# One pool for split weights and activations, a lookahead that depends on the place, and three pieces of work moved, in a two-layer hybrid encoder

## The chip, the cores and the metric

The kernel runs on one core of a Trainium2 chip. The time is the device time in microseconds (us) of one execution; the time of a kernel is the median of its runs. TensorE (PE) multiplies matrices, VectorE (DVE), ScalarE (ACT) and GpSimd (POOL) work element by element, and SyncE (SP) only issues DMAs. PEld is TensorE's loading of weights into its array, which runs beside its matmuls. PSUM, where the matmuls accumulate, has 8 banks of 128 x 512 float32; everything else lives in SBUF.

## The reference, cut to what matters

The input is 256 tokens of 1024 float32 values; two layers run one after the other, each with a gated feed-forward network (FFN), two kinds of attention with a common projection, and a second FFN.

```python
def swiglu(h, w_gate, w_up, w_down):
    return (jax.nn.silu(h @ w_gate) * (h @ w_up)) @ w_down

def reference(x, ...):
    for l in range(2):
        x = x + 0.5 * swiglu(rms_norm(x, ffn1_norm[l]), ffn1_w_gate[l], ffn1_w_up[l], ffn1_w_down[l])
        h = rms_norm(x, mix_norm[l])
        qa, ka, va, qb, kb, vb = jnp.split(h @ w_in[l], SPLITS, axis=-1)
        ...
        out_a = windowed_gqa_sink(qa, ka, va, sink[l], slopes_a)      # softmax with a sink, 8 heads, keys up to 128 away
        out_b = differential_attention(qb, kb, vb, lam, slopes_b)     # softmax1 - lam * softmax2, 4 heads
        out_b = rms_norm(out_b, diff_subln[l]) * (1.0 - lam_init)
        x = x + jnp.concatenate([out_a, out_b], axis=-1) @ w_out[l]
        x = x + 0.5 * swiglu(rms_norm(x, ffn2_norm[l]), ffn2_w_gate[l], ffn2_w_up[l], ffn2_w_down[l])
    return rms_norm(x, final_norm)
```

The hidden width of an FFN, `D_FF`, is 2816. `lam` comes from four short vectors per layer; `slopes` are powers of two.

## The kernel before, in words

**Split operands.** A float32 matrix product is made from three products of a faster type (float32r, written fp32r in the profile): each operand is split into `hi`, its rounded value, and `lo`, what the rounding left, and x·w is taken as xh·hi + xl·hi + xh·lo. So each piece of a product is three matmuls into one PSUM bank (`tokens`, L495; `prod`, L589). ScalarE makes `hi` by a copy, VectorE `lo` by a subtraction (`emit_split`, L175).

**Weight steps.** All weights are listed in advance, in the order of their use, as `specs`: one step is 1 MB, in an FFN 4 blocks of 128 rows by 512 columns. SP loads a step into one of 6 raw buffers (`emit_dma`, L147; the tiles `raw`). It is split in two halves (a half split), each into two buffers `w` of 128 x 2 x 512, from 14 such buffers (L181). `weights()` (L232) is called where a step is used. It first calls `ahead`, which issues all loads, preparations and splits up to half split 2i + HALVES, where i is the step and HALVES is 14 // 2 - 1 = 6, less a number that may be given. When the second half of a step is first touched, `part` (L166) lets `ahead` go one half further, unless the step is `held`. `ahead` is thus what places the splits in the queues of ScalarE and VectorE, among the other work.

**The order.** Every engine keeps the order in which the program issues (class `Kept`, L40), except in the first part of `mix`, where `kept[0]` is False and a scheduler chooses it. An instruction that waits holds up everything behind it on its engine.

**One FFN pass** (`ffn`, L567; four of them: two layers by two). Token blocks are t = 0, 1 of 128 tokens, and the 2816 hidden columns are groups n = 0 to 4 of 512 and a rest of 256. A group computes gate and up (each over 8 blocks of 128 rows of the input), silu by ScalarE, their product `h` by VectorE (`hidden`, L583); the next group turns `h` (`turn`, L634: transposes by TensorE, then a split as above) and multiplies it by the down weights of its group into four banks `accs` that stay for the whole pass (`down`, L648). So 4 of the 8 banks are left for the rest. Groups 0 and 1 are plain. Groups 2, 3 and 4 (`SEVEN`) get gate and up together by seven products in place of eight, in the manner of Strassen (`by_seven`, L599): m1, m7, p2, p3, p5, p6 and p4 in this order, with the halves of h's down product between. Sums of weights for them come from a gather-add DMA issued by POOL (`gather`, L125: c into b, b into a) and from additions by VectorE (`plus`, L130). Sums of x come from `make_sums` (L332), called in pieces through `next(sums, None)` in group 1. The differences of the products (`put`, L604, tiles `tmp`) are VectorE's; g1, the last of them that frees a bank, reads the bank of p4 (L623).

**Work around it.**

- `operands` (L311) splits x, transposed and scaled by the gain, into `xs`; `copies` (L322) makes a plain copy of the same banks by eight ScalarE operations, needed only by `make_sums`. It comes at the end of `take_x(2)` in the first pass (L430) and of `Residual.late(2)` in the others (L565), both called as `before(2)` in `ffn` (L662), before group 0's second half. The banks of the transposes are held until then.
- `constants` (L452) issues eight small DMAs, an iota and small operations on POOL, for the attention. `attention_constants` (L475) is the rest of these: a transpose of the gains into `gcol`, distances, and from `lsum` by an Exp on ScalarE (`lex`) the `nlam`: one transpose by TensorE, 11 operations of VectorE, one of ScalarE. It is `ffn`'s `aside`, called in the first pass at the start of n = 3 (L669). In the last pass `aside` is `final_gain` (L969), a load by SP and a memset.
- `blk` (L77) takes buffers for activations (xs, h, turned h, queries, keys) from the pool `s4` of 14, of the same size in bytes as a `w`.
- `mix` (L739) projects, does both attentions and the output projection; `ffn_end` and `ffn_close` (L700, L720) finish a pass and begin the next norm.

Of the kernel before, what the change touches and what calls it, by code (L numbers as in the profile page):

```python
# [10 lines left out]
F32R = mybir.dt.float32r  # L11
# [14 lines left out]
BIG = 1e33  # L26

AHEAD = 10
N_RAW, N_W = 6, 14
N_S4 = 14  # L30
SEVEN = (2, 3, 4)


# [1 line left out]
def trunk(ctx: ExitStack, tc: tile.TileContext, x, n1, g1, u1, d1, nm, w_in, sink,  # L35
# [31 lines left out]
    def nm_(s):  # L67
        uid[0] += 1
        return f"{s}_{uid[0]}"
# [90 lines left out]
    class Split:  # L160
# [5 lines left out]
        def part(self, k, c=slice(None), h=None):  # L166

            if h is None:
                h, k = divmod(k, 2)
            if h and not self.held:  # L170
                self.held = True
                ahead(2 * self.i + 1 + HALVES)
            return [t[:, k, c] for t in self.parts[h]]

    def emit_split(i, j):  # L175
        s = specs[i]
        raw = raws[s.src]
        if j == 0:
            loaded[i] = Split(i)
        shape = (P, 8, P) if s.n == 256 else (P, 2, 512)  # L180
        hi, lo = [wp.tile(list(shape), F32R, tag="w", bufs=N_W, name=nm_("w")) for _ in range(2)]  # L181
        loaded[i].parts.append((hi, lo))
        if s.n == D:
            raw = raw[:, :, j * 512:(j + 1) * 512]
        elif i in paired:
            raw = raw.rearrange("p k (s c d) -> p c k s d", s=2, c=2)[:, j]
            hi, lo = [t.rearrange("p k (s d) -> p k s d", s=2) for t in (hi, lo)]
        elif s.n == 256:
            raw = raw[:, :, j * P:(j + 1) * P]
        else:  # L190
            raw = raw[:, 2 * j:2 * j + 2]
        m = shape[1] // 2 if i < 2 or i in fine else shape[1]
        for a in range(0, shape[1], m):
            r_, h_, l_ = [t[:, a:a + m] for t in (raw, hi, lo)]
            act.copy(h_, r_)
            dve.tensor_tensor(l_, r_, f(h_), op=ALU.subtract)
            if i < 2:
                yield
        if j == 1:
            for k in s.free:  # L200
                raws.pop(k)
# [3 lines left out]
        for j in range(2):  # L205
            yield from emit_split(i, j)

    HALVES = N_W // 2 - 1
    at = dict(use=0, dma=2, prep=2, split=4)

    def ahead(n):

        n = min(n, 2 * len(specs) - 1)
        while True:
            if at["split"] <= n and at["prep"] > at["split"] // 2:
                for _ in emit_split(*divmod(at["split"], 2)):
                    pass
                at["split"] += 1
            elif at["prep"] <= min(n // 2 + 1, len(specs) - 1) and at["dma"] > at["prep"] and \
                    (specs[at["prep"]].prep is None or at["split"] >= 2 * at["prep"]):  # L220
                if specs[at["prep"]].prep is not None:
                    specs[at["prep"]].prep()
                at["prep"] += 1
            elif at["dma"] < min(at["use"] + AHEAD, len(specs)) and (specs[at["dma"]].moves is None or len(raws) < N_RAW):
                if specs[at["dma"]].moves is not None:
                    for _ in emit_dma(at["dma"]):
                        pass
                at["dma"] += 1
            else:
                break  # L230

    def weights(less=0, held=False):  # L232

        i = at["use"]
        at["use"] += 1
        if i > 1:
            ahead(2 * i + HALVES - less)
        w = loaded[i]
        w.held = held
        return w  # L240
# [168 lines left out]
    def take_x(k):  # L409

        g, u = early
        if k == 0:
            for j in (0, 1):
                sl = norm.turn(j)
                next(g)
                norm.operands(j, sl)
                next(u)
        elif k == 1:
            for e in (g, u, g, u):
                next(e)  # L420
            norm.pair(2)
            ahead(5)
            norm.pair(3)
        elif k == 2:
            ahead(7)
            for t in range(2):
                for h in range(2):
                    norm.squares(t, h * 512, 512)
            norm.stats()
            norm.copies()  # L430
            constants()

    grow = const.tile([NG - 16, P], F32, name="grow")
# [108 lines left out]
    class Residual:  # L542
# [14 lines left out]
        def late(self, k):  # L557

            if k == 1:
                self.nxt.pair(2)  # L560
                self.nxt.pair(3)
                self.squares(1)
            elif k == 2:
                self.nxt.stats()
                self.nxt.copies()  # L565

    def ffn(norm, aside=None, before=None, final=False):  # L567
        def silu(out_, acc, t):
# [30 lines left out]
        def by_seven(h, g):  # L599


            flat = lambda: tmp().rearrange("p a n -> p (a n)")

            def put(o, x, y, op):  # L604
                dve.tensor_tensor(o, x, y, op=op)
                return o

            m1, m7 = flat(), flat()
            act.copy(m1, prod(norm.quarter(0, 0), weights()))
            act.copy(m7, prod(norm.summed(2), weights(held=True)))  # L610
            hT = turn(h, 2)
            p2 = prod(norm.quarter(0, 1), weights())
            g0 = put(flat(), p2, m1, ALU.add)
            p3 = prod(norm.summed(3), weights())
            silu(g0, g0, 0)
            down(hT, g - 1, 0, weights())
            h = blk(F32)
            p5 = prod(norm.summed(0), weights())
            p6 = prod(norm.summed(1), weights())
            u2 = put(flat(), p6, m1, ALU.subtract)  # L620
            u3 = put(m7, m7, u2, ALU.add)
            p4 = prod(norm.quarter(1, 1), weights())
            g1 = put(m1, p4, u3, ALU.subtract)  # L623
            w = weights()
            silu(g1, g1, 1)
            put(u3, u3, p5, ALU.subtract)
            put(u2, u2, p5, ALU.subtract)
            put(u2, u2, p3, ALU.add)
            up(h, u2, g0, 0)
            up(h, u3, g1, 1)  # L630
            down(hT, g - 1, 1, w)
            return h
# [19 lines left out]
        gs, us = [bank(), bank()], [bank(), bank()]  # L652
        if before is None:
            before = norm.late
        before(0)
        ws = (weights(), weights(2))
        for k in (0, 2):
# [8 lines left out]
        h = hidden(g, us)  # L666
        for n in range(1, NGRP):
            sums = norm.make_sums() if n + 1 == min(SEVEN, default=0) else iter(())
            if n == 3 and aside is not None:  # L669
                aside()  # L670
            if n in SEVEN:
                h = by_seven(h, n)
                continue
            gs = [bank(), bank()]
            tokens(gs, norm.xs, weights(), 0)
            hT = turn(h, 2)
            tokens(gs, norm.xs, weights(), 4)
            g = gate(gs)
            next(sums, None)
            us = [bank(), bank()]  # L680
            for k0 in (0, 4):
                tokens(us, norm.xs, weights(), k0)
                next(sums, None)
            h = hidden(g, us)
            for hh in range(2):
                down(hT, n - 1, hh, weights())
                if hh == 0:
                    next(sums, None)

        gu = [bank(), bank()]  # L690
        tokens(gu, norm.xs, weights(), 0)
# [8 lines left out]
    def ffn_end(parts, last):  # L700

        accs, hT, rest = parts
        hT = [None] * (2 * (NGRP - 1)) + hT
        hE = []
        w = {0: weights()}

        def group(h, order, a=None, c=slice(None), first=0):
            tokens(a or accs[h], hT, w[h], G4, first=first, last=last[h], order=order, cols=c)

        def tail(h, order=BY_TOKENS, a=None, c=slice(None)):  # L710
            tokens(a or accs[h], [None] * (2 * NGRP) + hE, w["rest"], 4 * NGRP, last=last[h], order=order, cols=c, h=h)

        group(0, [(k, t) for k in range(3) for t in range(2)])
        hE.extend(rest())
        group(0, [(3, t) for t in range(2)])
        w["rest"] = weights()
        w[1] = weights(2)
        return group, tail

    def ffn_close(parts, nxt):  # L720
        group, tail = ffn_end(parts, (FC - 1, G4 + 3))
        res = Residual(nxt, parts[0])
        group(1, [(0, t) for t in range(2)])
        tail(0)
        for t in range(2):
            res.add(0, t)
        tail(1)
        ahead(2 * at["use"] - 2 + HALVES)
        group(1, [(1, t) for t in range(2)])
        for j in range(2):  # L730
            nxt.pair(j)
        res.squares(0)
        group(1, [(2, t) for t in range(2)])
        group(1, [(3, t) for t in range(2)])
        for t in range(2):
            res.add(1, t)
        nxt.late = res.late
# [318 lines left out]
```

## Time and profile before

| | |
|---|---|
| runs | 944.03, 944.5 and 947.19 us; median 944.5 |
| the profiled execution | 946.16 us |
| its span in the trace | 944.4 us |
| granted TensorE clock, mean | 0.993 |
| TensorE in the pieces `ps<-w,s` of 512 columns | 2754 matmuls, 645.4 us, 392 ns each |
| split of weights on VectorE, `w<-raw,w` | 440 operations, 464.1 us, 1094 ns each |
| split of weights on ScalarE, `w<-raw` | 440 operations, 399.1 us, 949 ns each |
| DMA | 194.59 MB, mean 206 GB/s |

The profile is of one execution. Its span runs from the first to the last instruction; the device time holds a little more around it. A matmul's record lasts longer than the distance to the next one, because matmuls are pipelined, so the records overlap and a busy share near the whole span does not say how fast the matmuls follow each other. In a group's line stand engine, line, operation, output tile <- input tiles, and their shapes; every instruction goes through the helper at L50, so tiles, not lines, tell the work apart. Behind a group may stand, in brackets, how long the engine was idle before it and what ended that.

### The profile page before, as it was taken

The numbers are of one execution on the slowest core, as the hardware profiler recorded it, in microseconds if no ns is written. First come the engines' busy times: TensorE is split into PE (matmuls) and PEld (weight loads), VectorE is DVE, ScalarE is ACT, GpSimd is POOL, SyncE is SP. The second block draws the span as 40 slices with busy tenths as digits, with TensorE's granted clock in tenths as the row PEclk, the third lists the DMA queues.
The fourth block names the chain that finished last, engine by engine and source line by source line (L and its number), as shares of the span: only waits on it lengthen the run. The fifth ranks groups of instructions, "written<-read, shape, count | busy, mean of one in ns | idle before, by whom it ended". The sixth has DMA issues, their size and how long they took to land.

```text
span 944.4 us, 12947 instructions
## 1 busy us (share of the span) xinstructions
PE 924.9 (98%) x4796; PEld 783.5 (83%) x4796; DVE 762.2 (81%) x1066; ACT 582.2 (62%) x901; POOL 53.6 (6%) x73
## 2 busy tenths in 40 slices
PE   8999899999999999999999999999999999999997
PEld 6788688899898888887888888878999888888876
DVE  6679999869955678999866799996796556799993
ACT  6756576467735756675575566665676475575662
POOL 0500010000000000000000010000000000010001
PEclk9999899999999999999999999999999999999999
DMA  9986797836424875897658498886652348499821
GB/s 336 345 222 182 218 277 255 271 120 194 134 90 134 233 213 141 263 295 265 239 178 235 122 278 223 259 296 195 194 161 90 130 157 249 103 286 268 254 93 45
DMA packets 110895, 194.59 MB, mean 206 GB/s; under 512 B 3566, under 2 KB 31280, under 8 KB 110832
## 3 DMA queue, kind: packets, MB, share of 16 engines
q1 hardware_dynamic: 96816, 167.27, 52.2%
q0 software_dynamic: 12928, 25.46, 15.1%
q10 hardware_dynamic: 1088, 1.05, 0.3%
q8 instruction: 37, 0.61, 0.3%
q14 instruction: 26, 0.21, 0.1%
HBM read 192.71 MB, written 1.05 MB: 205 GB/s over the span
## 4 chain that ended last, share of the span: by engine, by line
PE 83%; DVE 7%; DMA 5%; issue 2%; ACT 2%; ACTq 0%; DVEq 0%; POOLq 0%; POOL 0%
PE ps L50 83%; DVE w L50 5%; DMA raw<-in_ffn_w_up_dram 3%; DVE tmp L50 1%; ACT w L50 1%; DMA raw<-in_ffn_w_gate_dram 1%; DMA xk<-in_x_dram 1%; DVE s L50 1%; DVE raw L50 0%; ACT s L50 0%; ACT junk L50 0%; ACT tmp L50 0%; ACT L50 0%; ACTq L50 0%; DVE xk L50 0%
## 5 line engine op out<-in xcount | busy, mean ns | idle before, releaser
L50 PE MATMUL ps<-w,s 128*128 128x512 f32 (+1 forms) x2754 | 645.4, 392 | 7.1 <-DVE tmp L50 3.5
L50 PEld LDWEIGHTS ps<-w,s 128*128 128x128 f32 x2754 | 514.0, 189 | 115.2 <-DVE tmp L50 4.8
L50 DVE TENSOR_TENSOR w<-raw,w 128x1024 fp32r<-128x1024 f32 (+1 forms) x440 | 464.1, 1094 | 86.9 <-ACT w L50 84.1
L50 ACT CAST w<-raw 128x1024 fp32r<-128x1024 f32 (+1 forms) x440 | 399.1, 949 | 189.7 <-PE ps L50 97.1
L50 PE MATMUL ps<-w,q 128*128 128x512 f32 x432 | 101.9, 389 | 0.0
L50 PEld LDWEIGHTS ps<-w,q 128*128 128x128 f32 x432 | 81.1, 188 | 16.8
L50 PE MATMUL ps<-s,w 128*128 128x256 f32 x672 | 84.0, 285 | 0.0
L50 PEld LDWEIGHTS ps<-s,w 128*128 128x128 f32 x672 | 81.7, 192 | 1.1
L50 DVE TENSOR_TENSOR raw<-raw,raw 128x1024 f32<-128x1024 f32 x48 | 56.5, 1218 | 0.0
L50 POOL DMA_DIRECT2D raw<-in_ffn_w_up_dram x24 | 31.0, 1293 | 364.4 <-DVE tmp L50 157.2
L50 DVE TENSOR_TENSOR s<-ps,s 128x512 fp32r<-128x512 f32 x48 | 31.0, 685 | 18.1 <-ACT s L50 18.1
L50 ACT ACTIVATE s<-ps,gcol 128x256 fp32r<-128x256 f32 (+1 forms) x80 | 31.3, 476 | 20.7 <-PE ps L50 20.7
L50 ACT CAST s<-ps 128x512 fp32r<-128x512 f32 x48 | 26.1, 594 | 28.1 <-PE ps L50 28.1
L50 PE MATMUL ps<-ident,s 128*128 128x128 f32 x304 | 39.9, 273 | 1.7 <-DVE s L50 1.7
L50 PEld LDWEIGHTS ps<-ident,s 128*128 128x128 f32 x304 | 35.0, 141 | 6.9 <-ACT w L50 1.8
L50 ACT ACTIVATE s<-s,negm 128x256 f32<-128x256 f32 x64 | 31.8, 500 | 6.6 <-DVE negm L50 6.6
L50 ACT ACTIVATE tmp<-tmp,r 128x512 f32<-128x512 f32 x24 | 17.3, 722 | 29.2 <-DVE tmp L50 29.2
L50 PE MATMUL ps<-w,v 128*128 128x512 f32 x144 | 34.6, 389 | 0.0
L50 PEld LDWEIGHTS ps<-w,v 128*128 128x128 f32 x144 | 27.2, 189 | 5.7
L50 DVE SCALAR_TENSOR_TENSOR s<-ps,gcol,s 128x256 fp32r<-128x256 f32 x48 | 20.3, 479 | 14.4 <-ACT s L50 14.3
L50 DVE TENSOR_TENSOR tmp<-ps,tmp 128x512 f32<-128x512 f32 x36 | 24.6, 684 | 0.0
L50 DVE TENSOR_TENSOR tmp<-tmp,ps 128x512 f32<-128x512 f32 x36 | 23.6, 683 | 0.4
(107 smaller groups left out, 407.0 us busy)
## 6 DMA issues: line engine op xcount, KB each, us to landing
raw<-in_ffn_w_down_dram SPq DMA_DIRECT2D x44, 1024.0 KB, 5.2
raw<-in_ffn_w_gate_dram SPq DMA_DIRECT2D x39, 1024.0 KB, 5.4
raw<-in_ffn_w_up_dram SPq DMA_DIRECT2D x39, 1024.0 KB, 5.1
raw<-in_ffn_w_up_dram POOLq DMA_DIRECT2D x24, 1024.0 KB, 10.7
raw<-in_w_in_dram SPq DMA_DIRECT2D x14, 1024.0 KB, 5.7
raw<-in_ffn_w_gate_dram SPq DMA_DIRECT2D x8, 512.0 KB, 6.7
raw<-in_ffn_w_up_dram SPq DMA_DIRECT2D x8, 512.0 KB, 7.7
raw<-in_w_in_dram SPq DMA_DIRECT2D x8, 512.0 KB, 5.1
```

The costliest lines, as they stand in the source:

```text
L50: ins = issue(*a, **k)
```

## The change

- One pool of 28 buffers, tag `s4`, takes the place of the 14 buffers `w` and the 14 of `s4`: split weights and activations share it. The number of bytes is the same.
- `HALVES` = 6 becomes `look[0]`: 6 at the end of a pass and in `mix`, 8 in an FFN up to group 2, 7 in group 3 and 6 in group 4.
- In group 4 the steps of p6, p4 and the second down product are asked for with `less`, so that `ahead` goes only to half splits 2i+5, 2i+4 and 2i+3, and those of p6 and p4 are `held`. Splits that stood ahead of g1 in the queues come behind it, some after the calls that follow.
- `norm.copies()` goes from the end of `before(2)` to group 1, behind the turn of group 0's h.
- `aside()` goes from the start of n = 3 to group 1, behind the first down product of group 0 and the piece of `make_sums` that follows it. In the first pass that is `attention_constants`, in the last `final_gain`.

```diff
-N_RAW, N_W = 6, 14
-N_S4 = 14
+N_RAW, N_S4 = 6, 28
+IN_FFN, IN_MIX = 8, 6
...
-                ahead(2 * self.i + 1 + HALVES)
+                ahead(2 * self.i + 1 + look[0])
...
-        hi, lo = [wp.tile(list(shape), F32R, tag="w", bufs=N_W, name=nm_("w")) for _ in range(2)]
+        hi, lo = [s4.tile(list(shape), F32R, tag="s4", name=nm_("w")) for _ in range(2)]
...
-    HALVES = N_W // 2 - 1
+    look = [IN_MIX]
...
-            ahead(2 * i + HALVES - less)
+            ahead(2 * i + look[0] - less)
...
             norm.stats()
-            norm.copies()
             constants()
...
                 self.nxt.stats()
-                self.nxt.copies()
...
-            p6 = prod(norm.summed(1), weights())
+            late = g == max(SEVEN)
+            p6 = prod(norm.summed(1), weights(look[0] - 5 if late else 0, late))
             u2 = put(flat(), p6, m1, ALU.subtract)
             u3 = put(m7, m7, u2, ALU.add)
-            p4 = prod(norm.quarter(1, 1), weights())
+            p4 = prod(norm.quarter(1, 1), weights(look[0] - 4 if late else 0, late))
             g1 = put(m1, p4, u3, ALU.subtract)
-            w = weights()
+            w = weights(look[0] - 3 if late else 0)
...
+        look[0] = IN_FFN
         before(0)
...
-            if n == 3 and aside is not None:
-                aside()
             if n in SEVEN:
+                look[0] = IN_FFN - max(0, n - 2)
                 h = by_seven(h, n)
                 continue
...
             hT = turn(h, 2)
+            norm.copies()
...
                 down(hT, n - 1, hh, weights())
                 if hh == 0:
                     next(sums, None)
+                    if aside is not None:
+                        aside()
+                        aside = None
...
+        look[0] = IN_MIX
         w = {0: weights()}
...
-        ahead(2 * at["use"] - 2 + HALVES)
+        ahead(2 * at["use"] - 2 + look[0])
```

## The prediction, made before the changed kernel ran

> **What bounds the kernel now.** I read the page first, then the waits of TensorE alone, then busy time by stage, and last the timeline around each gap. The page says that TensorE sets the time:
>
> ```profile
> PE 924.9 (98%) x4796; PEld 783.5 (83%) x4796; DVE 762.2 (81%) x1066; ACT 582.2 (62%) x901; POOL 53.6 (6%) x73
> ```
>
> The waits of TensorE are few (total, count, longest, in us):
>
> ```profile
> PE ps L50 <- DVE tmp L50: 3.5, 3, 1.2
> PE ps L50 <- ACT tmp L50: 3.5, 1, 3.5
> ...
> PE ps L50 <- DVE s L50: 1.7, 2, 1.4
> ```
>
> So no change to the buffers can win more than these gaps and what the clock loses after them. The windows (length, busy of each engine with its instructions, granted clock, DMA share, GB/s) show that loss, and how full VectorE is:
>
> ```profile
> 39.60:43.00 3.40, 3.40 (x10) 2.62 (x9) 3.34 (x4) 1.40 (x2) 1.30 (x1) 0.51 1.05 401
> 109.30:114.70 5.40, 5.40 (x13) 4.24 (x14) 5.39 (x6) 5.19 (x7) 0.00 (x0) 0.51 0.00 0
> 340.00:350.00 10.00, 10.00 (x46) 8.29 (x45) 7.88 (x10) 4.98 (x6) 1.28 (x1) 1.00 0.70 154
> 430.00:440.00 10.00, 10.00 (x45) 7.98 (x44) 9.94 (x10) 6.39 (x7) 0.00 (x0) 1.00 0.66 226
> ```
>
> In dense stretches matmuls of 512 columns start 0.227 us apart (24 in 5.44 us). At a clock of 0.51 only 13 start in 5.40 us where 24 would: 11 x 0.227 = 2.5 us lost. In 39.6 to 43.0 it is 10 for 15: 1.1 us. VectorE has a fifth of its time free in group 1 (340 to 350) and none in group 4.
>
> **The three kinds of gap.** First pass, end of group 0:
>
> ```profile
> 26.22 3.00 ACT L50 ACTIVATE s<-ps,gcol 128x256 f32<-128x256 f32 x8
> ...
> 32.42 1.27 ACT L50 ACTIVATE tmp<-ps,r 128x512 f32<-128x512 f32 x2
> ...
> 36.94 1.40 DVE L50 SCALAR_TENSOR_TENSOR s<-ps,hr,tmp 128x512 f32<-128x512 f32 x2
> ...
> 37.83 0.30 PE L50 MATMUL ps<-ident,s 128*128 128x128 f32 x1 [1.43 <-DVE s L50]
> ```
>
> The eight copies of x stand ahead of the silu; the transposes wait for h. First pass, after group 2, where the constants sit:
>
> ```profile
> 103.88 0.18 DVE L50 COPY gcol<-ps 128x34 f32<-128x34 f32 x1
> ...
> 106.68 0.20 ACT L50 ACTIVATE lex<-lsum 128x4 f32<-128x4 f32 x1 [5.35 <-DVE lsum L50]
> ...
> 108.67 0.57 ACT L50 COPY tmp<-ps 128x512 f32<-128x512 f32 x1
> ...
> 109.30 2.93 PE L50 MATMUL ps<-w,s 128*128 128x512 f32 x6 [3.52 <-ACT tmp L50]
> ```
>
> ScalarE stands 5.35 us at lex, behind it the copy of m1 that frees a bank for TensorE. Passes 2, 3 and 4, end of group 4 (444, 624 and 905 us; pass 2 shown):
>
> ```profile
> 437.35 6.90 DVE L50 TENSOR_TENSOR w<-raw,w 128x1024 fp32r<-128x1024 f32 x6
> ...
> 444.17 0.68 DVE L50 TENSOR_TENSOR tmp<-ps,tmp 128x512 f32<-128x512 f32 x1
> ...
> 447.76 0.68 DVE L50 TENSOR_TENSOR tmp<-ps,tmp 128x512 f32<-128x512 f32 x1
> ...
> 448.50 3.70 PE L50 MATMUL ps<-w,s 128*128 128x512 f32 x15 [1.16 <-DVE tmp L50]
> ```
>
> g1 (447.76) reads p4's bank, which the last group's second accumulator needs; eight half splits stand ahead of it since the last prep.
>
> **The change part by part.** A half split is one cast (1.05 us) and one subtraction (1.22 us, next one 1.15 us later: 6 in 6.90).
>
> *Constants to group 1.* The same 11 VectorE operations, one transpose, the table load and lex. They leave the full stretch: the gap of 3.52 us goes, 0.16 us with it (a record lasts 0.39 us where starts are 0.227 apart, so a gap costs 0.16 more than it shows), and the 2.5 us of slow clock: -6.2 us. Where they go, VectorE waits at gcol until TensorE is through the first half of group 0's down projection (62.6 us by the timeline), then works from gcol to lsum's end 2.8 us and to the last nlam 3.5 us. ScalarE waits for lex behind it, with the splits of steps 13 and 14 and m1's and m7's copies queued. Step 12 is split before; TensorE has 5.4 us of step 9 and 2 x 2.7 us of steps 10 and 11 to do: cover until 73.7 us. Another wait lies in front: step 11 (b) receives a gather-add by POOL, issued at 43.85 and landed 55.58, and its cast now comes two halves earlier, at about 52.6, so ScalarE can stand there some 3 us. From 55.6: two casts and q to 59.7, h, step 12, v and the table to 67.5, lex at 69.9, four casts to 73.8, m1's copy 74.4, where p2 wants its bank at 74.6. That is no margin. VectorE then enters the full stretch about 1 us later against TensorE than in the other passes, whose tightest spot (h of group 3, 0.2 to 0.8 us before the transposes) gains only one half, 1.15 us. I take +0.5 us; bounds 0 (the gather lands by 53: the fastest of the page's first 100 us took 8.1 us) and +3.5 us (all of the constants' time comes out at TensorE).
>
> *Lookahead 8 in place of 6 halves, out of one pool.* VectorE does two half splits, 2 x 1.15 = 2.3 us, before group 2, in group 1's free time (2.1 us in 10). No work is added. In pass 1 they go ahead of h: step 5 is split before the squares, whose load landed at 24.07, 0.6 us after ScalarE is free at 23.43, and 2.0 us of casts follow.
>
> *Copies of x later.* 3.0 us leave ScalarE's queue ahead of silu, but the 0.6 + 2.0 us just named take their place: silu starts 0.1 us earlier at most, which is less than these rows can tell. So silu stays near 32.4, h near 36.9, and the first gap stays: 0. Bounds: 0 and the whole gap, 1.43 + 0.27 + 1.1 = -2.8 us. In group 1 the copies hold four banks until 41.6 (first two) to 43.1; the up projection needs the first at 46.3 in pass 1. In pass 2 they run 327.4 to 330.4 and the bank is needed at 331.6, the first being free at 328.1. Covered by 24 matmuls; if the copies came after that, each us late is a us of TensorE. POOL's constants start after the statistics, so 2.7 us later, still ending about 43.8 us, when it is due at the gather.
>
> *Group 4's differences up.* Three half splits fewer stand ahead of g1, and two were done early: 5 x 1.15 = 5.75 us earlier, 442.0 for 447.76, where the bank is wanted at about 447.0 (p4 ends by 441). Three gaps go: 1.16 + 1.20 + 1.19 + 3 x 0.16 = -4.0 us. Next late would be p4's weights, which in pass 2 arrive as they are used (438.06); they come 2.3 us earlier. The deferred splits follow h at 447.1 for a use near 452.6, so are hidden. Bounds: -4.0 and 0.
>
> *Projection and attention.* Nothing in mix is changed by a line, but the recorded order differs: six small splits move behind the keys, so VectorE stands idle for up to 3.7 us at 207.8. In the timeline queries and keys are ready 1.9 to 3.5 us before TensorE reads them, and VectorE has 1.6 us free in 220 to 230. I take 0; bounds -0.5 and +2 us for both layers. The final gain's load moves ahead on SP behind a wait for group 1's matmuls; SP's next loads are late by less than the 0.4 us of one issue: 0.
>
> Sum: -6.2 - 4.0 + 0.5 = -9.7 us. The profiled execution took 946.16 us for a span of 944.4 and is 1.7 us above the median of 944.5; 946.16 becomes 936.5, the median 934.8.
>
> **One rule against a row.** The gap of 1.43 and 0.27 us at 38 was followed by 3.4 us at half clock, the three gaps of 1.2 us by none. So by the rows a leftover gap of 1.7 us in pass 1 costs 1.1 us more, one of 1.2 us nothing. The Trainium skill, TensorE: Matmul & The Clock Gate, section "HAM oscillation — how this bites in real kernels", asks only for "no PE-idle gaps >~3.4µs"; by that a leftover gap of 1.7 us would cost itself alone. The row at 39.6 speaks against it here.
>
> **The rivals.** *The first gap goes too*: if step 5's cast does not fill the copies' place. For it: copies are 3.0 us of the 10.6 us before h. Against: the landing at 24.07. 934.8 - 2.8 = 932.0.
> *The constants' time comes out later in pass 1*: the gather and lex line up before m1's copy, without margin. +3.5 for +0.5, with 1.1 us of clock: 938.9.
> *The lookahead isn't reached*: loads or buffers are late, so the differences move but p4's weights hold TensorE instead, and the three gaps stay: 934.8 + 4.0 = 938.8. Against: raw buffers come free with the splits, so loads move up with them.
> *Slower: the copies hold the banks too long.* In each of four passes the up projection waits for them. It decides once the copies start over 3.5 us later than above (46.3 - 41.6 = 4.7 us in pass 1). If they then stand wholly in TensorE's way, 3.0 us and 1.1 us of clock, four times: 16.4 - 9.7 = +6.7, 951.2 us. For it: they stand in ScalarE's queue behind casts that wait for loads. Against: those loads landed at 32.2 and 35.6.
>
> **How the numbers follow.** Forecast 0.62; first gap too 0.09; constants later 0.13; lookahead not reached 0.07; banks 0.09. The likeliest gives 934.8. The forecast with its bounds holds 932.3 to 938.3; with the neighbours 931.5 to 940.5, which leaves out the banks and edges. A measurement tells no change within 0.3%, 2.8 us, so faster means below 941.7: all cases but the banks, and a few worst cases of constants and lookahead together: 0.87; between, 0.05; slower 0.08.
>
> **What would show it.** The wait <- ACT tmp gone and no slow clock near 108; the three <- DVE tmp gone; the 1.4 us before the transposes at 37.8 still there, with a slow clock after it; less than 1 us of waits in pass 1 after 60 us. A TensorE wait for ACT s at 46 or 331 would mean the banks; a wait for ACT tmp near 75, the constants; a wait for DVE w near 436, the lookahead. TensorE's waits lower by 7.1 us together (3.52 and the three gaps) would bear out the terms; a span over 938 the rivals.

## The result, and the profile after

| | before | changed |
|---|---|---|
| median of 7 runs each | 944.03 us (942.43 to 947.19) | 940.0 us (938.1 to 940.89) |
| ratio | | 0.9953, 95% interval 0.9937 to 0.9970 |
| the profiled execution | 946.16 us, span 944.4 | 938.1 us, span 936.3 |

The forecast was 934.8 us, 9.7 us less than before, with a range of 931.5 to 940.5. The medians differ by 4.0 us, four tenths of that. The two profiled executions differ by 8.1 us: the one before is 2.1 us above its median, the one after is the fastest of its seven. One trace of each kernel would have borne out most of the sum; the runs don't. What this trace hides is what the experiments had to find.

The busy times of the first profile after:

```profile
PE 922.1 (98%) x4796; PEld 782.2 (84%) x4796; DVE 757.3 (81%) x1066; ACT 573.2 (61%) x901; POOL 51.3 (5%) x73
```

TensorE's waits in it (total in us, count, longest):

```profile
PE ps L50 <- ACT tmp L50: 2.1, 1, 2.1
PE ps L50 <- DVE s L50: 1.3, 3, 0.7
```

The wait for the constants (3.5) and the three for DVE tmp are gone, as forecast. In their place one of 2.1 stands in group 1 of the first pass. Together these waits fell from 8.7 to 3.4 us, by 5.3 where the forecast asked for 7.1. ScalarE's and TensorE's rows around it (start, length, engine, instruction, and in brackets the idle time before it and what ended that):

```profile
24.22 2.00 ACT L50 CAST w<-raw 128x1024 fp32r<-128x1024 f32 x2 [0.71 <-DMA raw<-in_ffn_w_gate_dram]
26.12 0.62 ACT L50 ACTIVATE junk<-xk 128x512 f32<-128x512 f32 x1
...
29.01 1.98 ACT L50 CAST w<-raw 128x1024 fp32r<-128x1024 f32 x2
...
32.30 1.27 ACT L50 ACTIVATE tmp<-ps,r 128x512 f32<-128x512 f32 x2
...
33.04 7.33 PE L50 MATMUL ps<-w,s 128*128 128x512 f32 x24 [2.14 <-ACT tmp L50]
```

Step 5's casts stand ahead of the squares, the silu starts at 32.30 (32.42 before), and TensorE now stops earlier than at the transposes: group 1's gate needs a bank that the silu frees, because the copies of x still hold theirs. The windows (length, busy of each engine with its instructions, granted clock, DMA share, GB/s) at this place, where the constants were, and at the two places in the second pass shown before:

```profile
33.00:36.40 3.40, 3.36 (x8) 2.62 (x9) 1.87 (x2) 3.40 (x5) 3.06 (x15) 0.54 1.05 379
106.50:112.00 5.50, 5.45 (x28) 4.65 (x29) 5.50 (x6) 3.13 (x5) 0.00 (x0) 1.00 0.45 124
340.00:350.00 10.00, 10.00 (x46) 8.29 (x45) 8.37 (x11) 6.63 (x8) 0.00 (x0) 1.00 0.62 168
430.00:440.00 10.00, 10.00 (x46) 8.29 (x45) 9.97 (x11) 5.91 (x6) 0.00 (x0) 1.00 0.84 299
```

VectorE does one more operation in group 1 (11 for 10 in 340 to 350), and g1 of the second pass is early:

```profile
439.43 0.68 DVE L50 TENSOR_TENSOR tmp<-ps,tmp 128x512 f32<-128x512 f32 x1
```

That is 8.3 us ahead of 447.76: 3.4 us of it are TensorE's lead by then, by the starts of the same matmuls in both profiles, and 4.9 the move, for which 5.75 were worked out.

### The profile page after: what moved, and what is told of

Read it like the earlier page. It is cut to its first block, busy times and chain, and to the rows that moved or that the text cites. A ratio compares the mean times of both kernels' runs of the same rounds, so it can differ in the third digit from the quotient of the medians.

```text
span 936.3 us, 12676 instructions
## 1 busy us (share of the span) xinstructions
PE 922.1 (98%) x4796; PEld 782.2 (84%) x4796; DVE 757.3 (81%) x1066; ACT 573.2 (61%) x901; POOL 51.3 (5%) x73
## 3 DMA queue, kind: packets, MB, share of 16 engines
q10 hardware_dynamic: 1088, 1.05, 0.3%
HBM read 192.71 MB, written 1.05 MB: 207 GB/s over the span
## 4 chain that ended last, share of the span: by engine, by line
PE 92%; DMA 4%; DVE 1%; ACT 1%; issue 1%; SPq 0%; ACTq 0%; POOLq 0%; POOL 0%; DVEq 0%
PE ps L50 92%; DMA raw<-in_ffn_w_up_dram 2%; DMA raw<-in_ffn_w_gate_dram 2%; DVE w L50 1%; DMA xk<-in_x_dram 1%; ACT w L50 0%; DVE tmp L50 0%; ACT junk L50 0%; DVE s L50 0%; ACT tmp L50 0%; SPq L152 0%; ACT L50 0%; ACTq L50 0%; DVE xk L50 0%; POOLq L1056 0%
## 5 line engine op out<-in xcount | busy, mean ns | idle before, releaser
L50 ACT CAST w<-raw 128x1024 fp32r<-128x1024 f32 (+1 forms) x440 | 391.1, 948 | 85.8 <-DVE raw L50 71.0
L50 ACT CAST q<-tmp 128x512 fp32r<-128x512 f32 x20 | 12.4, 620 | 35.0 <-DVE tmp L50 34.9
L50 DVE TENSOR_TENSOR xk<-xk,ps 128x512 f32<-128x512 f32 (+1 forms) x25 | 14.2, 598 | 17.6 <-PE ps L50 17.6
```

Source lines behind the costliest of these rows:

```text
L50: ins = issue(*a, **k)
```

## The experiments

Below "before" is the kernel before the change, run on the same chip beside each experiment; each ratio is against it and has its 95% interval. The changed kernel's two sets of runs (14 in all) have a middle of 940.3 us; smaller differences of medians are taken against that. The sets come from three chips, on which the kernel before took 943.5 to 944.7 us, so a difference of under about a microsecond between two sets says nothing.

**One part undone at a time.** Constants back at the start of group 3:

```diff
+            if n == 3 and aside is not None:
+                aside()
...
-                    if aside is not None:
-                        aside()
-                        aside = None
```

> The changed kernel with the attention constants back at the start of group 3. Theory A (the gains are those that the two traces show, the smaller difference of the medians comes from the clock of single runs): the wait of TensorE for ACT tmp near 106 comes back with 3.5 us and half clock after it, the waits for DVE s at 105.9 and 137 go; the median is 3 to 5.5 us above the changed kernel's 940.0, so 943 to 945.5. Theory B (in a typical run the moved constants win little, since the time comes out later in the pass): within 1.5 us of 940.0.

941.51 us, ratio 0.9972 (0.9960 to 0.9983): 1.2 us above the changed kernel, and 1.5 above the 940.0 that the expectation started from, which is the edge of B: where the constants stand hardly matters here. Its trace has the wait of 3.3 us for the constants, and others of 0.9 at 72 and 2.3 us at 100, so the pass is late without them too.

Group 4 without the three half splits fewer:

```diff
-            late = g == max(SEVEN)
+            late = False
```

> The changed kernel without the smaller lookahead in group 4: the three half splits stand ahead of g1 again, the rest as changed. Theory A: g1 gains the lookahead's two half splits only, 2.3 us earlier, which is more than the gaps of 1.2 us, but the lookahead has shrunk to 6 by group 4, so nothing is gained: the three gaps of about 1.2 us return, 940.0 + 4.0 = 944. Theory B (the lookahead alone carries it): no gaps, 940.

942.22 us, ratio 0.9978 (0.9969 to 0.9988): 1.9 us above, halfway between the theories. A is refuted for its three gaps: one of them is left, with 0.4 us. But the trace has a wait that neither theory had:

```profile
PE ps L50 <- ACT tmp L50: 4.2, 1, 4.2
...
PE ps L50 <- DVE tmp L50: 0.4, 1, 0.4
```

It lies at 72 to 77 us, where TensorE wants the bank of m1, long before the place of the edit.

Copies of x back before group 0's second half:

```diff
             norm.stats()
+            norm.copies()
...
                 self.nxt.stats()
+                self.nxt.copies()
...
-            norm.copies()
             tokens(gs, norm.xs, weights(), 4)
```

> The changed kernel with the copies of x back before group 0's second half. The changed kernel's trace shows TensorE waiting 2.1 us for ACT tmp at 33.0. Theory A (the copies hold four banks, so group 1's gate waits for the silu; without that TensorE runs on to the transposes): the wait at 33 goes, the one for DVE s near 38 comes back with 3 us or more, since the copies and step 5's casts both stand ahead of the silu: 940.0 + 1 to + 3. Theory B (the banks cost more than the copies): 937 to 939.

939.97 us, ratio 0.9952 (0.9937 to 0.9966): no change. The wait at 33 went and one of 3.7 us before the transposes at 40.3 came, as A said; the time did not follow.

The silu of group 0 in the first pass ahead of the casts of steps 5 and 6:

```diff
-        look[0] = IN_FFN
+        first = before is take_x
+        look[0] = IN_MIX if first else IN_FFN
...
-        tokens(gs, norm.xs, weights(), 4)
+        tokens(gs, norm.xs, weights(3 if first else 0, first), 4)
         g = gate(gs)
+        look[0] = IN_FFN
```

> The changed kernel with group 0's silu in the first pass ahead of the casts of steps 5 and 6 in ScalarE's queue (squares, table load, silu, then casts); the rest as changed. Theory A (what is late at 33 is the silu, behind casts that wait for a load): the silu starts at about 27.7 in place of 32.3, the wait of 2.1 us and the half clock after it go, 2.3 to 3.4 us less: 936.6 to 937.7. Theory B (the transposes of h are next late, by the casts of step 5): a wait of 1 us or more near 38, 938.5 to 940.

940.8 us, ratio 0.9965 (0.9951 to 0.9980). A miss: the wait of 2.1 us at 33 is gone, and the time is not less. TensorE arrives at m1's bank earlier and waits 4.6 us there instead; the gather-add had also landed later, at 58.91 us. So the waits at 33 and at 75 are not two costs: something later sets when TensorE goes on.

**What sets it: the rival of the constants.** The changed kernel once more:

> The changed kernel once more, unedited, for another profile. Theory C (the constants' time comes out later in the first pass: whenever the gather-add into b lands after about 57 us, ScalarE's chain cast, q, cast, v, table load, lex, four casts ends after TensorE wants m1's bank): the gather-add lands at 57.5 us or later, TensorE waits 1.5 to 4.5 us for ACT tmp between 72 and 78, with half clock behind it where the wait is over 3 us, and the span is 938 to 939.5. Theory A (only the clock of single runs differs): no wait there over 1 us, as in the first profile of this kernel (936.3).

This execution took 941.02 us with a span of 939.2, and shows what the first profile did not (ScalarE's rows, then TensorE's):

```profile
57.84 2.00 ACT L50 CAST w<-raw 128x1024 fp32r<-128x1024 f32 x2 [5.74 <-DMA raw<-in_ffn_w_up_dram]
61.92 0.62 ACT L50 CAST q<-tmp 128x512 fp32r<-128x512 f32 x1 [2.08 <-DVE tmp L50]
62.45 2.00 ACT L50 CAST w<-raw 128x1024 fp32r<-128x1024 f32 x2
67.49 0.62 ACT L50 CAST v<-tmp 128x512 fp32r<-128x512 f32 x1 [3.04 <-DVE tmp L50]
68.13 1.28 ACT L50 ACT_TABLE_LOAD   x1
71.55 0.21 ACT L50 ACTIVATE lex<-lsum 128x4 f32<-128x4 f32 x1 [2.14 <-DVE lsum L50]
71.67 3.87 ACT L50 CAST w<-raw 128x1024 fp32r<-128x1024 f32 x4
75.44 0.57 ACT L50 COPY tmp<-ps 128x512 f32<-128x512 f32 x1
...
76.07 2.14 PE L50 MATMUL ps<-w,s 128*128 128x512 f32 x8 [2.81 <-ACT tmp L50]
```

ScalarE stands 5.74 us at b's cast, until the gather-add into b has landed (57.75 by its DMA row), and the rows behind it stand at the same distances from it as in the first profile, 17.6 us from b's cast to m1's copy in both. So the waits for VectorE in them are part of one chain. m1's copy starts 17.7 us after the landing. In the first profile it is the same 17.7 us (56.69 and 74.40), only that the landing was 1 us earlier and TensorE already late by the wait at 33: it came when the copy was done. That is theory C's trace in all its signs: a landing after 57.5, a wait between 1.5 and 4.5 us, a span within 938 to 939.5, and no half clock, which it expected only for a wait of over 3 us.

Exp of the lambda sums moved to the start of the first mix:

```diff
+    def lambdas():
         lex = const.tile([P, 2, DEPTH], F32, name="lex")
         act.activation(lex, lsum, AF.Exp)
...
+        if l == 0:
+            lambdas()
         kept[0] = False
```

> The changed kernel with the Exp of the lambda sums (lex, its table load, the three operations of nlam) taken out of the constants and put at the start of the first mix, on all engines in the written order. Theory C: ScalarE no longer stands 3.4 us for the table and lsum, m1's copy comes 3.4 us earlier, the wait near 75 is gone or under 1 us: 936 to 937.5, with less spread between runs. Theory A: within 1 us of 940.

938.59 us, ratio 0.9944 (0.9926 to 0.9961): 1.7 us less, between the two theories. The wait near 75 is gone; waits for VectorE of 0.9, 0.6, 0.7 and 0.3 us stand between 97 and 106 us, and the second profile of the changed kernel has the last three of them too.

The moves of the silu and of the Exp together:

> The changed kernel with lex at the start of the first mix and with group 0's silu in the first pass ahead of the casts of steps 5 and 6. Theory C: both waits (at 33 and near 75) go, the gather-add's landing (58 to 59 us) still sets m1's copy at about 73.5 where TensorE now comes at 72.2: a wait of 1 to 2 us is left: 935 to 936.5. Theory A: 937 to 938 (the wait at 33 alone).

939.73 us, ratio 0.9952 (0.9936 to 0.9968): a miss for both theories. With the early end of group 0, waits for VectorE of 0.6 to 1.1 us stand at four places between 37 and 107 us. The first pass as a whole was late, not one instruction. The starts of the same matmuls show how one delay hides another. The run with group 4's half splits back, after its wait of 4.2 us and half clock, was 3.4 us behind the second profile at 99 us, but met none of the waits for VectorE between 101 and 109 and was only 0.3 behind at 112.

**The lookahead.** 6 everywhere:

```diff
-IN_FFN, IN_MIX = 8, 6
+IN_FFN, IN_MIX = 6, 6
...
-                look[0] = IN_FFN - max(0, n - 2)
+                look[0] = IN_FFN
```

> The changed kernel with a lookahead of 6 everywhere, the rest as changed (in group 4 three half splits fewer still). Theory C: fewer loads run beside the gather-add, it lands near 55.6 to 56.5 as before the change, so the wait near 75 is under 1.5 us; step 5's casts leave the place ahead of the squares, so the silu comes 2 to 3 us earlier and the wait at 33 goes; the three waits at the end of group 4 stay away, as 3 x 1.15 us is more than 1.2: 936 to 938.5. Rival (the lookahead of 8 is what removes the waits in group 4): two or three waits of 0.5 us or more for DVE tmp, 940 to 943.

934.89 us (934.33 to 935.48), ratio 0.9901 (0.9882 to 0.9920): 5.4 us less than the changed kernel, and below both expectations. Its waits, after the start:

```profile
PE ps L50 <- DVE s L50: 1.0, 3, 0.3
```

The reason given for it was half wrong: the gather-add landed at 57.48 us, no earlier than in the first profile of the changed kernel (56.69). What differs is what stands behind it (ScalarE's rows):

```profile
57.55 2.00 ACT L50 CAST w<-raw 128x1024 fp32r<-128x1024 f32 x2 [3.37 <-DMA raw<-in_ffn_w_up_dram]
61.63 0.62 ACT L50 CAST v<-tmp 128x512 fp32r<-128x512 f32 x1 [2.08 <-DVE tmp L50]
62.27 1.28 ACT L50 ACT_TABLE_LOAD   x1
65.69 0.20 ACT L50 ACTIVATE lex<-lsum 128x4 f32<-128x4 f32 x1 [2.13 <-DVE lsum L50]
65.80 3.88 ACT L50 CAST w<-raw 128x1024 fp32r<-128x1024 f32 x4
69.58 0.57 ACT L50 COPY tmp<-ps 128x512 f32<-128x512 f32 x1
```

The third q and two casts are done before b's cast instead of after it, and m1's copy comes 12.1 us after the landing, not 17.7. At the start, too, step 5's casts no longer stand ahead of the squares; the two casts shown are the earlier pair that stands at 21.50 in the first profile:

```profile
20.00 2.00 ACT L50 CAST w<-raw 128x1024 fp32r<-128x1024 f32 x2 [0.42 <-DMA raw<-in_ffn_w_gate_dram]
21.90 0.63 ACT L50 ACTIVATE junk<-xk 128x512 f32<-128x512 f32 x1
...
28.09 1.27 ACT L50 ACTIVATE tmp<-ps,r 128x512 f32<-128x512 f32 x2
```

The silu starts at 28.09, and TensorE runs through to the transposes at 35.75 without a wait.

6 in the first pass alone, 8, 7 and 6 in the others:

```diff
-        look[0] = IN_FFN
+        first = before is take_x
+        look[0] = IN_MIX if first else IN_FFN
...
-                look[0] = IN_FFN - max(0, n - 2)
+                look[0] = IN_MIX if first else IN_FFN - max(0, n - 2)
```

> The changed kernel with a lookahead of 6 in the first pass only; the other three passes keep 8, 7 and 6. Theory D (the lookahead of 8 costs in the first pass alone, where it puts casts that wait for a load ahead of the squares and ahead of one more of the sums of x): as with 6 everywhere, 934.9, give or take 0.8. Theory E (it costs in every pass, or the place doesn't matter): 937 to 940.

933.99 us, ratio 0.9890 (0.9875 to 0.9905): D, a tenth below its bounds. All of the cost is in the first pass. In this run the gather-add landed at 58.95 us and m1's copy again came 12.1 us later (71.06), without a wait of TensorE: the order decided, not the landing.

Then two runs that divide that pass: 6 in its groups 0 and 1 only, the rest as changed; and 8 there only, with 6 everywhere else.

> The changed kernel with a lookahead of 6 in groups 0 and 1 of the first pass only; from group 2 on 8, 7, 6 as changed. Theory F (the cost is made in groups 0 and 1, by casts placed ahead of the squares and of one more sum): as with 6 in the whole first pass, 934.0, give or take 0.8. Rival G (it is made in groups 2 to 4 of that pass): 938 to 940.

> A lookahead of 8 in groups 0 and 1 of the first pass alone, 6 everywhere else, the rest as changed. Theory F: all of the cost is back, 939 to 941. Rival G: 934 to 936.

936.78 us, ratio 0.9923 (0.9911 to 0.9936), and 938.13 us, ratio 0.9935 (0.9922 to 0.9947). The first differs from the run before it (933.99) by the lookahead in groups 2 to 4: 2.8 us. The second differs from the run with 6 everywhere (934.89) by the lookahead in groups 0 and 1: 3.2 us. Together that is 6.0, where both at once cost 6.3. So neither F nor G holds: about half of the cost is made in each part. With 8 in groups 0 and 1 alone the two waits for ACT tmp are back, 0.9 us at 32 and 1.3 us at 74, in a profile that is 2.9 us longer than with 6 everywhere. By the starts of the same matmuls all of that is there by 75 us, 0.6 us of it already at 10 us, before the lookahead can matter.

**The other parts, with the lookahead out of the way.** With 6 everywhere, one part undone each: the constants, the smaller lookahead in group 4, the copies, with the edits shown above.

> Lookahead 6 everywhere and the attention constants back at the start of group 3; copies and group 4 as changed. Theory D (the prediction's price for the constants holds once the lookahead is out of the way): the wait for ACT tmp near 100 is back with 3.5 us, 934.9 + 3.7 without half clock after it to + 6.2 with it: 938.6 to 941.1. Theory B (the move wins little): under 936.5.

939.51 us (937.23 to 940.54), ratio 0.9946 (0.9930 to 0.9961): 4.6 us above 934.89, as D has it. The wait and the window behind it look as before the change:

```profile
PE ps L50 <- ACT tmp L50: 3.8, 1, 3.8
```

```profile
105.60:111.00 5.40, 5.38 (x13) 4.23 (x14) 5.38 (x6) 5.20 (x7) 0.00 (x0) 0.50 0.00 0
```

> Lookahead 6 everywhere and group 4 without the three half splits fewer; the rest as changed. Theory D (the smaller lookahead in group 4 is worth its 4.0 us where no lookahead of 8 has already worked ahead): three waits of about 1.2 us for DVE tmp return at the ends of group 4 in the second, third and fourth pass: 938.9. Rival (g1 is on time anyway, as it was with 8): 935 to 936.

941.42 us (940.19 to 944.14), ratio 0.9971 (0.9959 to 0.9983): 6.5 us above, more than D's 4.0. The waits returned, in all four passes, the first included:

```profile
PE ps L50 <- DVE tmp L50: 5.0, 4, 1.3
```

> Lookahead 6 everywhere and the copies of x back before group 0's second half; the rest as changed. Theory D (the copies' 3.0 us stand ahead of the silu when step 5's casts don't): the gap before the transposes at 37.8 returns with 1.4 + 0.3 us, with or without 1.1 us of half clock: 936.7 to 937.9. Rival (their place is nothing): 934.9.

934.75 us, ratio 0.9898 (0.9883 to 0.9912): nothing, D refuted. Of the gap before the transposes 0.4 and 0.3 us came back, and no more. The place is not free, though: by the starts of the same matmuls 1.05 us are lost there (38 us) against the run with 6 everywhere, and 1.1 us are taken back by 133 us, where that run waits for h and this one does not.

**The best version.** 6 in the first pass, 8, 7 and 6 in the others, and the Exp at the start of the mix:

> Lookahead 6 in the first pass, 8, 7, 6 in the others, and lex with its table load at the start of the first mix. Theory F (without the early casts there is slack of some 2 us at m1's copy, so lex's 3.4 us cost little): only the waits of 0.3 us each at 133 can go, 933.0 to 934.2. Rival (lex still sets m1's bank in most runs): 931 to 932.5.

933.72 us (933.12 to 934.13), ratio 0.9889 (0.9873 to 0.9904). That beats the kernel before by 10 us and the changed one by 6.6, and can't be told from the version without the Exp's move (933.99). After the start its TensorE waits half a microsecond:

```profile
PE ps L50 <- DVE s L50: 0.5, 2, 0.3
```

## Why the prediction was wrong

**The step that failed: "Lookahead 8 in place of 6 halves".** It was entered with "No work is added" and no cost. Against 6 in the same kernel it costs 5.4 us everywhere (940.3 to 934.89) and 6.3 us in the first pass alone. The counting was right, since no instruction is added; what went unpriced is the order. A split issued two halves earlier is not only done earlier; where its data come by a late DMA it stops ScalarE, and all that is queued behind it, earlier. Both places were in the prediction's working: step 5's casts ahead of the squares, and b's cast two halves earlier with the constants behind it. The first was priced at nothing, on the ground that it only took the copies' place. The second was given as +0.5 us with the words "That is no margin", with +3.5 as its bound. A third place, too, was entered as free: the two half splits were to be done in group 1's idle time of VectorE. With a lookahead of 8 VectorE starts 53 subtractions of weights ahead of group 2's h (both profiles of the changed kernel), before the change and with 6 it is 51.

The second profile against the trace of before, by the starts of the same matmuls, shows what that did to the sum: 1.7 us ahead at 60 us, 1.6 behind at 77, 3.1 behind at 104, 1.7 ahead at 115. So the constants' old place gave 4.8 us for the 6.2 forecast, while 3.3 us were lost at m1's bank and 1.5 at the waits for VectorE, places for which the sum had +0.5 together.

**The rival that came nearest.** *The constants' time comes out later in pass 1*, 938.9 us, with a chance of 0.13. Its place (m1's copy at 74.4) and its mechanism (the gather and lex in line) are what the second profile shows, without the half clock that it added; its time lies between the forecast and the measured median. It is a part of the miss only: with the Exp out of the line the kernel gained 1.7 us. The +0.5 rested on one landing, 55.58 us in the trace of before; the landings under the changed order were 56.69, 57.75 and, in its variants with a lookahead of 8 there, 57.2 to 58.9; in the variants with 6 they were 55.6 to 59.0, so the lookahead doesn't set the landing. A step "without margin" should have been priced with the whole wait.

**The constants, -6.2 us.** Right in kind, on the condition that the lookahead is 6: 4.6 us as the median of six runs. In the profile with the constants back 7.0 us are lost between 99 and 108 us, by the starts of the same matmuls, and 1.2 of them taken back by 133, where TensorE then doesn't wait for h. The quickest of the six, 937.23 us, has a mean clock of 0.999 where the others have 0.994 or 0.995, so it probably went without the half clock. With 8 the move is worth 1.2 us, because the pass is late anyway.

**Group 4, -4.0 us.** The three waits of 1.2 us went, each at its size. With a lookahead of 6 the step is worth 6.5 us: the first pass has a fourth such wait, 1.23 us at 161, that the trace of before didn't show, presumably because TensorE was later there. Four waits of 1.25 and 0.16 us make 5.6 of it; 0.9 us remain unexplained. With 8 it is worth 1.9 us by the medians (1.0 and 1.4 us by the starts from 160 us on, against the two profiles of the changed kernel), and its profile has hardly a wait there: VectorE's earlier work removes the same waits. The two parts of the change overlap, and the prediction added them as if they didn't.

**Copies, 0 us.** Right with either lookahead: with the copies put back the medians are 0.3 and 0.1 us lower. The banks they hold did stop TensorE, at 33 in the first pass, and nowhere else; the slower rival was not met. The prediction looked for that at the up projection (46.3) and missed that group 1's gate needs a bank earlier.

**First gap, kept.** It stayed, as 2.1 us at 33 instead of 1.7 before the transposes, for the reason given: the silu came no earlier. With 6 it goes, so its place among the rivals was tied to the wrong part, the copies.

**Projection and attention, 0.** By the starts of the same matmuls in the two profiles, each of the two mixes lost 0.4 us. That is inside the bounds.

With the lookahead of 6 the kernel takes 934.89 us, a tenth from the 934.8 forecast. That closeness is luck: there the first gap is gone too, and the two large terms, taken out one at a time, are worth 4.6 and 6.5 us where 6.2 and 4.0 were entered.

What stays open in part: how the lookahead of 8 in groups 2 to 4 of the first pass makes its 2.8 us. The profile of that run has waits of 0.9 us at 72 and of 0.8 and 0.3 us for group 2's h at 103 to 104. That h is late by VectorE: it starts at 102.74 with 53 subtractions of weights before it, against 100.37 with 51 where the whole pass has 6, and two subtractions are 2 x 1.15 = 2.3 us. The starts of the same matmuls give 1.7 us of the 2.8 by 160 us in this pair of profiles; no trace shows the rest.

## What to carry to other kernels

In a queue that keeps its order, an earlier place is not free even where no work is added: ask of each operation that moves up whether its data are there by then, and price what stands behind it with the whole wait if there is no margin. Depth of lookahead can be set by place, and is best kept short where the loads themselves are late, as in the first pass. Time lost at one late operand can be taken back at the next, so taking away an early wait may win nothing. Parts of a change that remove the same wait don't add, and one trace of each kernel may differ by twice what the medians do; so measure parts with the others both in and out.

## What the runs showed of the hardware

Half clock after a gap is not fixed by the gap's length. It came after 1.43 and 0.27 us (before, at 38), after 2.14 (changed, at 33) and after 3.52, 3.66, 3.80, 4.19 and 4.61 us; it did not come after 2.25 and 3.30 us (constants back) nor after 1.57 and 2.81 us (the changed kernel again). This window of that second profile begins with the end of the same wait at 33 that was followed by a clock of 0.54 in the first:

```profile
32.60:36.00 3.40, 3.34 (x14) 2.74 (x15) 1.85 (x2) 3.40 (x6) 3.06 (x15) 1.00 1.06 380
```

14 matmuls at full clock where the other had 8, 6 x 0.227 = 1.4 us, so the same place may cost that or nothing. The prediction took such a loss from one trace (2.5 and 1.1 us) as fixed. The Trainium skill, TensorE: Matmul & The Clock Gate, section "What's actually happening", says that the clock's window of about 3.4 us runs freely and doesn't start with the work; the rows here fit that: each of the gaps over 3.4 us listed above was followed by half clock, the shorter ones only at times. So a gap need not reach 3.4 us to cost it: 2.14 us was enough once, and 3.30 us was not.
